# The state chain of an RWKV-7 / dilated attention layer: chain steps issued with a raised priority, the other VectorE and ScalarE work of a step behind the step's two copies

## The chip, the cores and the metric

One core of a Trainium2 chip runs the whole layer in one launch. The metric is the device time of one execution in microseconds (us), median of three runs. Four engines matter: TensorE (PE in the profile; its weight loads are a row of their own, PEld), VectorE (DVE), ScalarE (ACT) and GpSimd (POOL). Each takes its instructions in the order in which the built program has them. SyncE (SP) issues most DMAs.

## What is computed

A decoder layer on 1024 tokens of width 1024, all in float32. One RMS norm and one input projection feed two branches: 16 heads of RWKV-7 time mixing, and 16 heads of attention over three dilated windows. Both are gated by SiLU, joined by one output projection, added to the input and normed again. The change touches only the recurrence of the time mixing:

```python
def rwkv7_time_mix(p_shift, gate, w0, w_up, a0, a_up, k_k, k_a, r_k, ln_x_w, ln_x_b):
    ...
    def step(state, inp):
        r_t, w_t, k_t, v_t, av_t, bv_t = inp
        sa = jnp.einsum('bhvk,bhk->bhv', state, av_t)
        state = (state * w_t[:, :, None, :] + sa[..., None] * bv_t[:, :, None, :]
                 + v_t[..., None] * k_t[:, :, None, :])
        return state, jnp.einsum('bhvk,bhk->bhv', state, r_t)
    ...
    _, y = lax.scan(step, s0, xs)
    ...

def reference(x, norm_w, w_in, mu_shift, ...):
        xn = rms_norm(h, norm_w)
        p = jnp.einsum('bsd,dn->bsn', xn, w_in.astype(jnp.float32))
        ...
        y_rwkv = rwkv7_time_mix(...)
        y_att = mixed_dilated_attention(p[..., ATT0:ATT_GATE0], p[..., ATT_GATE0:])
        mix = jnp.concatenate([y_rwkv, y_att], axis=-1)
        h = h + jnp.einsum('bsm,md->bsd', mix, w_out.astype(jnp.float32))
    return rms_norm(h, final_norm_w).astype(x.dtype)
```

## The kernel before

**Stages.** `rwkv` (L291) does the time mixing, then `attention` and `project_out` follow. The input projection is one long stream of 128x512 matmuls (`stream`, tiles `pq`, L187; three products per weight tile, since each float32 factor is split in two). It is a generator, and every stage draws a few of its matmuls between its own work (`advance`).

**Units and slots.** The time mixing is cut into 16 units: 8 pairs of heads times 2 halves of the sequence, each unit 8 chunks of 64 tokens. The loop over `p` at L341 works on four units at once: unit p+2 is prepared (`prepare`, `products`), p+1 is inverted (`late`, `invert`), p is chained (`chain`), p-1 is finished (`finish`). An iteration has 24 slots (`NSLOT`). A slot runs the steps put into it, the chain step first, then draws 4 matmuls of the projection.

**The chain.** A unit has 24 chain steps, three per chunk. Each ends in a pair of copies out of PSUM: VectorE takes head 0, ScalarE takes head 1, ScalarE behind VectorE.

- `first`: `z<-Sd` (state times keys), copies to `zd`; then two matmuls into `T` that no step waits for at once.
- `second`: `z<-zd` with the inverted matrix `U`, copies to `ud`, scaled by `rn`.
- `third`: `T<-ud`, copies to `Sd`, scaled by the decay: the state of the next chunk. Then `z<-Vd` opens the next `z`.

So a chain step is: matmul, VectorE copy, ScalarE copy, next matmul. The copies are L654 and L655 (`zd`), L657 and L658 (`ud`, `Sd`).

**The inversion.** `U` of a unit comes from `invert`: 15 columns of small VectorE operations (L568, L570: tiles `TB`, `UB`), a trip through DRAM (L577, L581), then four rounds m1 to m4 of small matmuls with ScalarE copies behind each (m1: L596, L599; m2: L606, L610 and the VectorE transpose L611; m3: L619, L622; m4: L628, L631). The second chain step of a unit, `z<-zd`, reads `U`, so it can't run before the last copy of m4.

**What sets the order.** The program is traced in the order of the slots, and a list scheduler then places it: on each engine it takes, of what is ready by its own reckoning of time, the instruction with the highest priority, and priority is the order of tracing. The engines then run that list in order. The lines that this hangs on:

```python
                if dC:
                    put(enumerate(self.chain(dC, get(p + 1) if dC["h"] == 0 else None)))
                ...
                for s in range(NSLOT):
                    for f in ev[s]:
                        f()
                    self.advance(n)
```

Of the kernel before, what the change touches and what calls it, by code (L numbers as in the profile page):

```python
# [12 lines left out]
AF = mybir.ActivationFunctionType  # L13
# [16 lines left out]
ATTG0 = 7296  # L30
NSLOT = 3 * NC_
AHEAD = 120
OFILL = 8
WARM = (4, 0)
V_AT = (-2, 3, -1)
# [18 lines left out]
class Kern:  # L54
# [135 lines left out]
    def stream(self, jobs):  # L190
# [3 lines left out]
        for i, (_, halves, take) in enumerate(jobs):  # L194
# [9 lines left out]
                yield  # L204
            w = wn

    def advance(self, n):
        for _ in range(n):
            next(self.flow, None)
        self.taken += n  # L210
# [80 lines left out]
    def rwkv(self, pairs=range(NPAIR), apairs=range(NPAIR)):  # L291
        nc = self.nc
        with ExitStack() as ctx:
            P = lambda n, b=1, s=None: self.pool(n, b, s, ctx)
            self.ps_a = P("ps_a", 1, PSUM)
            self.ps_z = P("ps_z", 1, PSUM)
            self.ps_y = P("ps_y", 1, PSUM)
            self.ps_tr = P("ps_tr", 1, PSUM)
            self.mid = P("mid", 2)
            self.inv = P("inv", 1)  # L300
            self.pers = pers = P("pers")
            self.lng = P("lng", 3)
            self.dpool = P("dpool", 2, bass.MemoryType.DRAM)
            self.carry = pers.tile([128, 25], F32, name="carry")
            self.Us = [pers.tile([128, NC_ + 1, C], F32, name=f"U{i}") for i in range(2)]
            self.Vds = [pers.tile([128, NC_, 2, HD], F32, name=f"Vd{i}") for i in range(2)]
            self.Sds = [pers.tile([128, 2, HD], F32, name=f"Sd{i}") for i in range(2)]
            self.llo = [pers.tile([128, 128], F32R, name=f"llo{i}") for i in range(2)]
            self.zds, self.uds = ([pers.tile([128, 2, HD], F32, name=f"{nm}{i}") for i in range(2)] for nm in ("zd", "ud"))
            for u in self.Us + self.Vds + self.Sds + self.zds + self.uds:  # L310
                nc.gpsimd.memset(u, 0.0)
            for u in self.llo:
                nc.gpsimd.memset(u.bitcast(F32), 0.0)
            self.ARs = [pers.tile([128, NC_ * 192 + 2], F32, name=f"AR{i}") for i in range(3)]
            for a in self.ARs:
                nc.gpsimd.memset(a[:, NC_ * 192:], 0.0)
                a = self.c192(a)
                for e in range(2):
                    er = slice(e * 64, e * 64 + 64)
                    nc.gpsimd.tensor_copy(out=a[er, :, 0], in_=bc(self.ident[er, er].unsqueeze(1), (64, NC_, 64)))  # L320
            self.d0 = pers.tile([128, 2, C + 1], F32, name="d0")
            nc.gpsimd.memset(self.d0, 1.0)
            nc.gpsimd.memset(self.d0[:, :, C:C + 1], 0.0)
            bank = lambda p, tag: lambda: p.tile([128, 4, 128], F32, name="xq", tag=tag)
            ba = [bank(self.ps_a, "pa0"), bank(self.ps_a, "pa1")]
            tags = ("MV", "MV", "MV", "TU", "TU", "BK")
            for _ in self.prep_x(0, self.lng, tags, [bank(self.ps_proj, "proj")] * 2 + ba):
                pass
            units = [dict(h=h, pr=pr) for pr in pairs for h in range(2)]
            for i, d in enumerate(units):  # L330
                d["AR"], d["Vd"] = self.ARs[i % 3], self.Vds[i % 2]
            N = len(units)
            self.flow = self.stream(self.jobs(units, apairs))
            next(self.flow)
            self.taken = 1
            self.params(self.lng.tile([P_N, 128], F32, name="rows", tag="TU"),
                        self.ps_tr.tile([128, P_N], F32, name="prm_ps", tag="tr"))
            self.advance(6 * KT - 1)
            get = lambda n: units[n] if 0 <= n < N else None
            self.lora_w(units[0])  # L340
            for p in range(-2, N):  # L341
                dA, dI, dC, dF = get(p + 2), get(p + 1), get(p), get(p - 1)
                ev = [[] for _ in range(NSLOT)]
                put = lambda steps: [ev[s].append(f) for s, f in steps]
                if dC:
                    put(enumerate(self.chain(dC, get(p + 1) if dC["h"] == 0 else None)))
                if dF:
                    put(self.finish(dF))
                if dI:
                    put(self.late(dI))  # L350
                    put(self.invert(dI, self.Us[(p + 1) % 2]))
                if dA:
                    lag = WARM[p + 2] if p < 0 else 0
                    put([(n + lag, f) for n, f in self.prepare(dA) + self.products(dA)])
                if get(p + 3) and get(p + 3)["h"] == 0:
                    ev[12].append(lambda d=get(p + 3): self.lora_w(d))
                elif get(p + 3):
                    get(p + 3)["lw"] = get(p + 2)["lw"]
                if p == -2:
                    px = self.prep_x(1, self.lng, tags, ba)  # L360
                    for s in range(4):
                        ev[s].append(lambda: [next(px, None) for _ in range(2)])
                    ev[4].append(lambda: [None for _ in px])
                n = 5 if p < 0 else 2 if dA is not None and get(p + 3) is None else 4
                for s in range(NSLOT):
                    for f in ev[s]:
                        f()
                    self.advance(n)
            for _, f in self.finish(units[-1]):
                f()  # L370

# [262 lines left out]
    def chain(self, d, nxt):  # L634


        nc = self.nc
        V, S, G = nc.vector, nc.scalar, nc.gpsimd
        h, pr = d["h"], d["pr"]
        er = [slice(0, 64), slice(64, 128)]  # L640
        t = {}
        f2 = lambda ap: ap.rearrange("p a b -> p (a b)")
        mm = lambda out, w, x, start, stop: nc.tensor.matmul(out, lhsT=w, rhs=f2(x), start=start, stop=stop,  # L643
                                                             skip_group_check=True)

        def values(c):

            t["z"] = self.ps_z.tile([128, 2, 128], F32, name="z")
            mm(t["z"][0:66, 0], d["MV"][:, c * 192 + 128:c * 192 + 194], d["Vd"][:, c], True, False)

        def spread(out, q, scale):

            if scale is None:
                V.tensor_copy(out=out[er[0], 0], in_=q[0:64, 0:64])  # L654
                S.copy(out=out[er[1], 1], in_=q[0:64, 64:128])  # L655
            else:
                V.tensor_scalar(out=out[er[0], 0], in0=q[0:64, 0:64], scalar1=scale[0], scalar2=None, op0=ALU.mult)  # L657
                S.activation(out=out[er[1], 1], in_=q[0:64, 64:128], func=AF.Copy, scale=scale[1])  # L658

        def first(c):  # L660
            AR = d["AR"]
            if c == 0:
                values(c)
            if c % 4 == 0:
                d["T", c // 4] = self.ps_y.tile([128, 4, 128], F32, name=f"T{c // 4}")
            Sd, T, zd = self.Sds[c % 2], d["T", c // 4][:, c % 4], self.zds[c % 2]
            mm(t["z"][0:66, 0], AR[:, c * 192 + 128:c * 192 + 194], Sd, False, True)
            spread(zd, t["z"][:, 0], None)
            mm(T, d["MV"][:, c * 192:c * 192 + 128], d["Vd"][:, c], True, False)
            mm(T, AR[:, c * 192:c * 192 + 128], Sd, False, False)  # L670

        def second(c):
            mm(t["z"][0:66, 1], f2(d["U"])[:, c * 64:c * 64 + 66], self.zds[c % 2], True, True)
            spread(self.uds[c % 2], t["z"][:, 1], [d["rn"][0:64, c:c + 1], d["rn1"][:, c:c + 1]])

        def third(c):
            T = d["T", c // 4][:, c % 4]
            if c == 5:
                self.heads_out(d, 0)
            mm(T, f2(d["TU"][:, c])[:, 0:128], self.uds[c % 2], False, True)  # L680
            if c == NC_ - 1 and nxt is None:
                G.memset(self.Sds[0], 0.0)
                return
            dec, n = (nxt["dec"], 0) if c == NC_ - 1 else (d["dec"], c + 1)
            spread(self.Sds[(c + 1) % 2], T, [dec[:, e, n:n + 1] for e in range(2)])
            if n:
                values(n)
        return [lambda f=f, c=c: f(c) for c in range(NC_) for f in (first, second, third)]
# [411 lines left out]
```

## Time and profile before

| what | value |
|---|---|
| time, median of 3 runs | 1586.47 us (1586.15 to 1588.06) |
| the profiled execution: time, span | 1586.58 us, 1584.9 us |
| TensorE busy over the span | 1492.5 us (94%) |
| VectorE, ScalarE, GpSimd busy | 64%, 56%, 34% |
| granted clock | 0.993 of full speed |
| stage of the chain | about 128 to 875 us |

The chain stage takes nearly half of the span. The rows below are of that stage. A group of instructions "x2" on PE is one float32 matmul in two passes. The busy time of PE is modelled at its end and matmuls overlap, so the distance from one start to the next says more than the durations.

### The profile page before, as it was taken

To read this page: it belongs to the slowest core of one execution; us is meant where nothing else is said; L and a number is where in the kernel's file an instruction comes from. 1 tells how busy PE (TensorE), PEld (TensorE's weight loads), DVE (VectorE), ACT (ScalarE), POOL (GpSimd) and SP (SyncE) were. 2 spreads that over 40 slices of the span, in tenths; PEclk is the share of its full clock that TensorE was granted. 3 is DMA by queue.
4 is the path that set the end of the run, shared out by engine and by line. 5 is a ranking of instruction groups with operands and counts; after the bars stand their busy time and mean duration, and the time that the engine had idled before them with its cause. 6 is when DMAs were issued, how large, how long until landed. Compare 5 with 4: busy or idle time off the path is not lost.

```text
span 1584.9 us, 29112 instructions
## 1 busy us (share of the span) xinstructions
PE 1492.5 (94%) x10721; PEld 1211.0 (76%) x10721; DVE 1014.7 (64%) x2686; ACT 892.7 (56%) x2080; POOL 532.9 (34%) x668
## 2 busy tenths in 40 slices
PE   5889999999999999999999999999999999999997
PEld 4677777777777777777677788888888888787886
DVE  5866767677666676666743557676675766856234
ACT  5546666666656666566654456556565555645231
POOL 5443132222222221232211433443333334355542
PEclk9999999999999999999999999999999999999999
DMA  6121111111111111111111201111111111436452
GB/s 195 56 67 38 34 40 42 35 45 28 39 45 33 46 39 26 47 31 45 31 40 35 68 28 34 39 50 34 34 34 41 47 48 47 157 103 193 134 166 99
DMA packets 178829, 94.87 MB, mean 60 GB/s; under 512 B 58413, under 2 KB 164606, under 8 KB 178686
## 3 DMA queue, kind: packets, MB, share of 16 engines
q1 hardware_dynamic: 174942, 86.19, 19.6%
q10 hardware_dynamic: 3744, 6.82, 1.3%
q8 instruction: 84, 1.38, 0.4%
q14 instruction: 59, 0.48, 0.1%
HBM read 75.01 MB, written 17.83 MB: 59 GB/s over the span
## 4 chain that ended last, share of the span: by engine, by line
PE 66%; DVE 18%; ACT 9%; issue 4%; POOL 1%; DMA 1%; DVEq 0%; SPq 0%; ACTq 0%; POOLq 0%
PE pq L187 31%; PE oq L984 10%; PE T L643 4%; PE z L643 3%; PE o L930 3%; PE pa L527 2%; PE mp L857 2%; PE sp L890 2%; DVE I L422 1%; PE sp L910 1%; PE sp L909 1%; ACT zt L724 1%; DVE TB L568 1%; ACT ud L658 1%; DVE UB L570 1%
## 5 line engine op out<-in xcount | busy, mean ns | idle before, releaser
L187 PE MATMUL pq<-xh,wh 128*128 128x512 f32 x1040 | 430.6, 414 | 0.0
L187 PE MATMUL pq<-xl,wh 128*128 128x512 f32 x1040 | 414.7, 399 | 0.0
L187 PE MATMUL pq<-xh,wl 128*128 128x512 f32 x1040 | 291.8, 404 | 0.0
L179 POOL TENSOR_TENSOR wl<-wraw,wh 128x512 fp32r<-128x512 f32 x138 | 181.1, 1328 | 173.9 <-issue 46.3
L187 PEld LDWEIGHTS pq<-xh,wh 128*128 128x128 f32 x1040 | 197.0, 190 | 32.6 <-issue 0.2
L187 PEld LDWEIGHTS pq<-xl,wh 128*128 128x128 f32 x1040 | 197.4, 190 | 31.2 <-DVE xl L166 0.2
L187 PEld LDWEIGHTS pq<-xh,wl 128*128 128x128 f32 x1040 | 187.8, 190 | 33.0
L918 POOL TENSOR_TENSOR pl<-p,ph 128x512 fp32r<-128x512 f32 (+2 forms) x96 | 102.0, 1068 | 202.7 <-ACT ph L917 182.4
L984 PE MATMUL oq<-ow,qr 128*128 128x512 f32 x512 | 162.2, 395 | 1.2 <-ACT ow L965 0.6
L859 DVE CUSTOM_DVE_ANT_0 mp<-mp,maskq 128x512 f32<-128x512 f32 (+1 forms) x192 | 105.5, 570 | 68.0 <-PE mp L857 59.5
L913 ACT ACTIVATE p<-p 128x512 f32<-128x512 f32 (+2 forms) x144 | 64.6, 452 | 103.8 <-DVE p L912 103.0
L979 POOL TENSOR_TENSOR vr<-kr,qr 128x512 fp32r<-128x512 f32 (+2 forms) x68 | 90.4, 1335 | 80.9 <-ACT qr L978 74.0
L984 PEld LDWEIGHTS oq<-ow,qr 128*128 128x128 f32 x512 | 95.9, 188 | 23.0 <-ACT ow L965 1.0
L984 PE MATMUL oq<-ow,vr 128*128 128x512 f32 x256 | 101.2, 395 | 1.9 <-POOL vr L979 1.9
L178 ACT CAST wh<-wraw 128x512 fp32r<-128x512 f32 x138 | 79.7, 618 | 40.6 <-PE pq L187 30.9
L978 ACT CAST qr<-kr 128x512 fp32r<-128x512 f32 (+2 forms) x68 | 40.2, 594 | 94.3 <-PE oq L984 53.1
L912 DVE TENSOR_TENSOR p<-sp,maskt 128x512 f32<-128x512 f32 (+2 forms) x144 | 65.3, 457 | 42.9 <-PE sp L910 41.4
L643 PEld LDWEIGHTS T<-ud,TU 128*128 128x128 f32 x256 | 39.6, 188 | 56.2 <-ACT ud L658 51.8
L643 PE MATMUL T<-ud,TU 128*128 128x128 f32 x256 | 59.4, 314 | 22.7 <-ACT ud L658 22.1
L657 DVE TENSOR_SCALAR Sd<-T,dec 64x64 f32<-64x64 f32 x120 | 33.0, 275 | 66.8 <-PE T L643 65.0
L658 ACT ACTIVATE ud<-z,rn 64x64 f32<-64x64 f32 x128 | 39.4, 308 | 56.5 <-DVE ud L657 54.9
L658 ACT ACTIVATE Sd<-T,dec 64x64 f32<-64x64 f32 x120 | 36.9, 308 | 57.0 <-DVE Sd L657 55.6
(235 smaller groups left out, 3126.6 us busy)
## 6 DMA issues: line engine op xcount, KB each, us to landing
wraw<-in_w_in_dram SPq DMA_DIRECT2D x138, 256.0 KB, 3.0
kr<-mixd SPq DMA_DIRECT2D x60, 256.0 KB, 3.0
oraw<-in_w_out_dram SPq DMA_DIRECT2D x16, 512.0 KB, 5.2
xt<-in_x_dram SPq DMA_DIRECT2D x8, 512.0 KB, 3.8
ld<-TU SPq DMA_DIRECT2D x32, 128.0 KB, 2.7
mixd<-zt SPq DMA_DIRECT2D x16, 256.0 KB
mixd<-gt SPq DMA_DIRECT2D x16, 256.0 KB, 2.2
xr<-in_x_dram ACTq DMA_DIRECT2D x16, 256.0 KB, 2.8
```

Of the source, the lines that this page charges most:

```text
L178: nc.scalar.copy(out=wh[:, ks], in_=raw)
L179: nc.gpsimd.tensor_tensor(out=wl[:, ks], in0=raw, in1=wh[:, ks].bitcast(F32), op=ALU.subtract)
L187: return [lambda i=i, a=a, b=b: self.nc.tensor.matmul(q, lhsT=a, rhs=b, start=(i == 0), stop=(i == len(ops) - 1)) for i, (a, b) in enumera ...
L643: mm = lambda out, w, x, start, stop: nc.tensor.matmul(out, lhsT=w, rhs=f2(x), start=start, stop=stop, skip_group_check=True)
L658: S.activation(out=out[er[1], 1], in_=q[0:64, 64:128], func=AF.Copy, scale=scale[1])
L859: V.tensor_tensor_reduce(out=mp[:, :kn], in0=mp[:, :kn], in1=self.maskq[:, v0:v0 + kn], op0=ALU.add, op1=ALU.max, scale=1.0, scalar=-3e38, ...
L912: V.tensor_tensor(out=p[:, :qn], in0=sp[:, :qn], in1=self.maskt[:, u0:u0 + qn], op=ALU.add)
L913: S.activation(out=p[:, :qn], in_=p[:, :qn], func=AF.Exp)
L918: G.tensor_tensor(out=pl[:, :qn], in0=p[:, :qn], in1=ph[:, :qn].bitcast(F32), op=ALU.subtract)
L930: nc.tensor.matmul(oc, lhsT=v, rhs=w[:, :qn], start=(first and i == 0), stop=(last and i == len(prods) - 1), skip_group_check=True)
L979: nc.gpsimd.tensor_tensor(out=ml, in0=raw, in1=mh.bitcast(F32), op=ALU.subtract)
L984: nc.tensor.matmul(q, lhsT=m[:, i], rhs=v, start=(k == 0 and j == 0), stop=(k == 15 and j == 2))
```

## The change

Three edits. First, every chain step is traced under a priority raised by 90 places (`urgent`, `AHEAD_OF`), so that the scheduler treats its instructions as if they stood 90 instructions earlier. Second, the two copies of a chain step are kept (`self.copies`), and everything that the same slot traces behind the chain step on VectorE gets an ordering edge to the VectorE copy, and everything on ScalarE one to the ScalarE copy (`issue_after`): it may not stand ahead of that copy in its engine's list. The edge orders the issue and adds no wait. The draws of the projection in the slot (`advance`) are inside as well, so the `shift` and `gate` operations that they bring are held by the same edges; matmuls and GpSimd's work are not. Third, where a unit has no state copy (the last step of every second unit), the list of copies is empty.

```diff
+AHEAD_OF = 90
...
+    def urgent(self, f):
+
+        with self.tc.high_priority(offset=AHEAD_OF):
+            f()
...
                 if dC:
-                    put(enumerate(self.chain(dC, get(p + 1) if dC["h"] == 0 else None)))
+                    for s, f in enumerate(self.chain(dC, get(p + 1) if dC["h"] == 0 else None)):
+                        ev[s].append(lambda f=f: self.urgent(f))
...
                 for s in range(NSLOT):
-                    for f in ev[s]:
-                        f()
-                    self.advance(n)
+                    with ExitStack() as order:
+                        for i, f in enumerate(ev[s]):
+                            f()
+                            if dC and i == 0:
+                                for ins in self.copies:
+                                    order.enter_context(self.tc.issue_after(ins.ins))
+                        self.advance(n)
...
             if scale is None:
-                V.tensor_copy(out=out[er[0], 0], in_=q[0:64, 0:64])
-                S.copy(out=out[er[1], 1], in_=q[0:64, 64:128])
+                a = V.tensor_copy(out=out[er[0], 0], in_=q[0:64, 0:64])
+                b = S.copy(out=out[er[1], 1], in_=q[0:64, 64:128])
...
+            self.copies = [a, b]
...
             if c == NC_ - 1 and nxt is None:
+                self.copies = []
                 G.memset(self.Sds[0], 0.0)
                 return
```

No instruction is added or taken away on any engine: PE keeps 8051 matmuls, VectorE 2688 instructions, ScalarE 2084, GpSimd 673, SP 575. From the 4848th matmul on, the order on PE is the same again, so only the chain stage is another. Two places show how.

**A chain step in the middle of a unit (the fourth chunk of the seventh unit).** On PE before, the matmuls of steps `first` and `second` of this chunk (`T_4772` is the unit's first `T`, `bq` and `pa` are other units' work), with the line numbers of the kernel before:

```order
1223 L643 MATMUL z<-Sd_123,AR_142 66x128
1224 L643 MATMUL T_4772<-Vd_120,MV 128x128
1225 L643 MATMUL T_4772<-Sd_123,AR_142 128x128
1226 L506 MATMUL bq<-bh,bdr 128x512
1227 L506 MATMUL bq<-bl,bdr 128x512
1228 L187 MATMUL pq<-xh_79,wl 128x512 x6
1229 L643 MATMUL z<-zd_127,U_118 66x128
1230 L187 MATMUL pq<-xh_79,wl 128x512
1231 L527 MATMUL pa_5039<-AR_144,BK 128x128
1232 L527 MATMUL pa_5040<-AR_144,BK 128x128
```

Now, on PE at the same steps (the line numbers are 1 to 13 higher, `tq` and `zq` are other units' work):

```order
1239 L188 MATMUL pq<-xh_78,wh 128x512
1240 L654 MATMUL z<-Sd_123,AR_142 66x128
1241 L654 MATMUL T_4772<-Vd_120,MV 128x128
1242 L654 MATMUL T_4772<-Sd_123,AR_142 128x128
1243 L188 MATMUL pq<-xl_80,wh 128x512
1244 L654 MATMUL z<-zd_127,U_118 66x128
1245 L188 MATMUL pq<-xh_78,wl 128x512 x4
1246 L416 MATMUL zq<-lx_342,lhi_4516 128x512
1247 L417 MATMUL zq<-lx_342,llo_124 128x512
1248 L416 MATMUL aq<-lx_343,lhi_4517 128x512
```

Between `z<-Sd` and `z<-zd` stood two `bq` and six `pq`; one `pq` is left there, and four stand behind `z<-zd`.

On VectorE before, the small operations of the group norm (`rs_w`, `gr`) and `Y` stood behind the `zd` copy of this step and ahead of its `ud` copy:

```order
760 L654 COPY zd_127<-z 64x64
761 L449 RECIPROCAL rn<-rn 128x8
762 L78 TENSOR_TENSOR rs_w<-rs_w,rs_x 128x8
763 L79 SCALAR_TENSOR_TENSOR gr<-rs_w,gr 128x8
764 L77 TENSOR_TENSOR rs_w<-gr 128x8
765 L78 TENSOR_TENSOR rs_w<-rs_w,rs_x 128x8
766 L79 SCALAR_TENSOR_TENSOR gr<-rs_w,gr 128x8
767 L77 TENSOR_TENSOR rs_w<-gr 128x8
768 L78 TENSOR_TENSOR rs_w<-rs_w,rs_x 128x8
769 L79 SCALAR_TENSOR_TENSOR gr<-rs_w,gr 128x8
770 L713 TENSOR_TENSOR Y<-Y,gr 128x512
771 L657 TENSOR_SCALAR ud_129<-z,rn 64x64
```

Now small operations of the norm and of the inversion's columns (`TB`, `UB`) stand between the state copy (`Sd`) and the `zd` copy of the same step:

```order
751 L668 TENSOR_SCALAR Sd_123<-T_4772,dec 64x64
752 L78 TENSOR_TENSOR rs_w<-gr 128x8
753 L579 TENSOR_TENSOR TB<-UB,AB 64x28
754 L79 TENSOR_TENSOR rs_w<-rs_w,rs_x 128x8
755 L581 TENSOR_TENSOR UB<-UB,TB 64x14x2
756 L80 SCALAR_TENSOR_TENSOR gr<-rs_w,gr 128x8
757 L579 TENSOR_TENSOR TB<-UB,AB 64x15
758 L78 TENSOR_TENSOR rs_w<-gr 128x8
759 L581 TENSOR_TENSOR UB<-UB,TB 64x15
760 L79 TENSOR_TENSOR rs_w<-rs_w,rs_x 128x8
761 L80 SCALAR_TENSOR_TENSOR gr<-rs_w,gr 128x8
762 L665 COPY zd_127<-z 64x64
```

So ten small operations now stand ahead of the `zd` copy that feeds row 1244 of PE, and behind the `Sd` copy that feeds its row 1240; before, the nine of the group norm stood behind that `zd` copy.

**The end of the fifth unit and the start of the sixth.** On PE before, from m4 (the sixteen `x` matmuls) on:

```order
1002 L628 MATMUL x_4111<-U_119,Xs 32x32 x16
1003 L187 MATMUL pq<-xh_79,wh 128x512
1004 L187 MATMUL pq<-xl_81,wh 128x512
1005 L187 MATMUL pq<-xh_79,wh 128x512
1006 L187 MATMUL pq<-xl_81,wh 128x512
1007 L643 MATMUL z<-zd_127,U_118 66x128
1008 L187 MATMUL pq<-xh_79,wl 128x512 x6
1009 L643 MATMUL T_3909<-ud_129,TU 128x128
1010 L187 MATMUL pq<-xh_79,wl 128x512 x2
1011 L643 MATMUL z<-Vd_121,MV 66x128
1012 L643 MATMUL T_4182<-Vd_121,MV 128x128
1013 L496 MATMUL tq<-ident,BK 128x128 x4
```

Now, from m3 on:

```order
1037 L630 MATMUL x_4111<-UT,TU 32x32 x16
1038 L188 MATMUL pq<-xh_79,wh 128x512
1039 L188 MATMUL pq<-xl_81,wh 128x512
1040 L188 MATMUL pq<-xh_79,wh 128x512
1041 L188 MATMUL pq<-xl_81,wh 128x512
1042 L639 MATMUL x_4111<-U_119,Xs 32x32 x16
1043 L188 MATMUL pq<-xh_79,wh 128x512
1044 L188 MATMUL pq<-xl_81,wh 128x512
1045 L188 MATMUL pq<-xh_79,wh 128x512
1046 L188 MATMUL pq<-xl_81,wh 128x512
1047 L654 MATMUL z<-zd_126,U_119 66x128
1048 L188 MATMUL pq<-xh_79,wl 128x512 x6
```

Before, m4 stood ahead of the last steps of the old unit (`z<-zd_127`, `T<-ud_129`), and the reader of `U_119`, the `z<-zd` of the new unit, came 18 rows behind m4, in row 1020. Now the new unit's first `z<-Sd` is already done (its `T_4182` matmuls stand in rows 1022 and 1031), and the reader `z<-zd_126` stands four `pq` behind m4.

## Rows read from the trace of the kernel before

**Rows 1.** Windows: us, then busy time of each engine (instructions), PEclk, DMA share, GB/s

```profile
128.00:875.00 747.00, 703.78 (x6732) 551.73 (x6731) 493.38 (x1528) 455.46 (x1202) 183.07 (x308) 1.00 0.16 38
875.00:1584.90 709.90, 691.16 (x3351) 580.14 (x3349) 435.06 (x971) 368.44 (x744) 295.56 (x264) 0.99 0.25 76
```

**Rows 2.** Chain of waits, 400 to 450 us: start, us, nine `pq` in a row

```profile
447.87 2.09 PE pq L187 x9
```

**Rows 3.** Timeline, 420 to 434 us: start, us, instruction, count [idle before <-releaser]

```profile
426.14 0.17 DVE L77 TENSOR_TENSOR rs_w<-gr 128x8 f32<-128x8 f32 x1
...
426.34 0.17 DVE L78 TENSOR_TENSOR rs_w<-rs_w,rs_x 128x8 f32<-128x8 f32 x1
...
430.79 0.38 PE L643 MATMUL z<-Sd,AR 128*66 128x128 f32 x2
...
431.01 0.39 PE L643 MATMUL T<-Vd,MV 128*128 128x128 f32 x2
...
431.23 0.39 PE L643 MATMUL T<-Sd,AR 128*128 128x128 f32 x2
```

**Rows 4.** Timeline, 500.5 to 514 us: chain copies behind free engines

```profile
501.16 0.38 PE L643 MATMUL z<-zd,U 128*66 128x128 f32 x2
...
501.47 0.68 PE L596 MATMUL xq<-U,LT 32*16 32x16 f32 x64
501.58 0.28 DVE L657 TENSOR_SCALAR ud<-z,rn 64x64 f32<-64x64 f32 x1 [1.38 <-PE z L643]
501.89 0.31 ACT L658 ACTIVATE ud<-z,rn 64x64 f32<-64x64 f32 x1 [1.45 <-DVE ud L657]
...
510.62 0.38 PE L643 MATMUL z<-Sd,AR 128*66 128x128 f32 x2
...
511.04 0.22 DVE L654 COPY zd<-z 64x64 f32<-64x64 f32 x1 [0.41 <-PE z L643]
...
511.29 0.20 ACT L655 COPY zd<-z 64x64 f32<-64x64 f32 x1 [0.79 <-DVE zd L654]
```

**Rows 5.** Tile T, matmuls `T<-ud`: duration min/median/max in ns, first and last start

```profile
L643 PE MATMUL T<-ud,TU x256: 270/275/377, 132.3 to 874.8; 128*128 128x128 f32 x128
```

**Rows 6.** Waits of PE, 128 to 876 us: us in total, times, longest us

```profile
PE T L643 <- ACT ud L658: 22.1, 39, 1.0
PE z L643 <- ACT zd L655: 9.2, 11, 1.3
PE z L643 <- ACT Sd L658: 7.4, 15, 0.7
```

**Rows 7.** Timeline, 433 to 446 us: a late state copy

```profile
435.07 1.50 ACT L724 COPY zt<-yq 64x256 f32<-64x256 f32 x4
...
435.62 0.28 DVE L657 TENSOR_SCALAR Sd<-T,dec 64x64 f32<-64x64 f32 x1
...
436.82 0.81 ACT L461 ACTIVATE ta<-ta,hk 128x512 f32<-128x512 f32 x1
...
437.66 0.31 ACT L658 ACTIVATE Sd<-T,dec 64x64 f32<-64x64 f32 x1
...
438.02 0.43 PE L643 MATMUL z<-Sd,AR 128*66 128x128 f32 x2 [0.61 <-ACT Sd L658]
```

**Rows 8.** Timeline, 500.5 to 514 us: the rounds m2 to m4 of an inversion

```profile
506.04 1.06 ACT L610 COPY U<-dq 16x128 f32<-16x128 f32 x4 [0.44 <-PE dq L606]
...
507.13 0.71 DVE L611 STREAM_TRANSPOSE UT<-U 128x512 f32<-128x512 f32 x1 [0.98 <-ACT U L610]
...
509.75 0.76 ACT L622 COPY Xs<-x 32x256 f32<-32x256 f32 x2 [0.21 <-PE x L619]
...
511.38 0.69 PE L628 MATMUL x<-U,Xs 32*32 32x32 f32 x32
...
512.12 0.74 ACT L631 COPY U<-x 32x256 f32<-32x256 f32 x2 [0.62 <-PE x L628]
```

More of the change, by code (lines that the diff above doesn't have):

```diff
@@ L653, in spread @@
             if scale is None:
-                V.tensor_copy(out=out[er[0], 0], in_=q[0:64, 0:64])
-                S.copy(out=out[er[1], 1], in_=q[0:64, 64:128])
-            else:
-                V.tensor_scalar(out=out[er[0], 0], in0=q[0:64, 0:64], scalar1=scale[0], scalar2=None, op0=ALU.mult)
-                S.activation(out=out[er[1], 1], in_=q[0:64, 64:128], func=AF.Copy, scale=scale[1])
+                a = V.tensor_copy(out=out[er[0], 0], in_=q[0:64, 0:64])
+                b = S.copy(out=out[er[1], 1], in_=q[0:64, 64:128])
+            else:
+                a = V.tensor_scalar(out=out[er[0], 0], in0=q[0:64, 0:64], scalar1=scale[0], scalar2=None, op0=ALU.mult)
+                b = S.activation(out=out[er[1], 1], in_=q[0:64, 64:128], func=AF.Copy, scale=scale[1])
+            self.copies = [a, b]
         def first(c):
```

## The prediction, made before the change was timed

> **What bounds the kernel now.** I read the windows first, to see which engine fills the stage that the change touches, then the spacing of matmuls in the chain of waits and the timeline, then the tile view of the chain's matmuls, then PE's waits and the timeline around one of them.
>
> In the chain stage PE is busy 703.78 of 747.0 us (94%), VectorE 493 (66%), ScalarE 455 (61%); behind it PE is busy 691 of 710 us [rows 1]. From the 4848th matmul on the order is the same, so the change is worth what it does to the stage, and a us of PE there is a us of the end.
>
> How much of the stage is waiting? Starts tell more than busy time. A `pq` follows a `pq` after 2.09/9 = 0.232 us [rows 2], a chain matmul of two passes takes 0.22 [rows 3]. A change between these and the small matmuls of an inversion costs about 0.09 more: the second pass of `z<-zd` starts at 501.27, `xq` 0.20 later instead of 0.11 [rows 4]. I gave every matmul of the stage such a cost, the other kinds by their own starts. From the first `T<-ud` to the last, the order before holds 682 us of PE work; the trace takes 874.8 - 132.3 = 742.5 [rows 5]. So 60.6 us are waiting. The wait rows show 22.1 + 9.2 + 7.4 = 38.7 of it, all for the ScalarE copy that ends a chain step [rows 6]; the rest is gaps that modelled ends hide.
>
> [...]
>
> Why is a copy late? In one example the `Sd` copy on VectorE ends at 435.90, but its partner on ScalarE starts at 437.66: ScalarE was in four `zt` copies and `ta`, which its list had ahead. `z<-Sd` follows 0.05 us behind it and PE had stood 0.61 us [rows 7].
>
> With free engines a copy pair takes little. `z<-zd` at 501.16, VectorE at 501.58, ScalarE from 501.89 to 502.20, plus the 0.05: 1.09 us from one chain matmul to the next. For the lighter `zd` pair: 510.62 to 511.49, plus 0.05: 0.92 us [rows 4]. The order before gives 1.79 us of PE work a step (682 over 381), so on the mean there is time in hand; what counts is which steps have less.
>
> **The change part by part.** It adds and removes no instruction. What moves is the chain: it runs ahead of the other work until it meets the inversion. So it can be placed the moment its copies are reckoned ready, where before it often stood behind projection matmuls and had time in hand.
>
> *Cover.* For each of 360 steps (units 2 to 16; the first is startup) I counted from the order the PE work P between two chain matmuls, and the VectorE and ScalarE work D and A between the matching copies. A copy falls behind by the larger of D - P and A - P; the next step takes that up with P less 1.09 (or 0.92), and PE waits for what is left. An example is shown under the change: ten small VectorE operations 0.20 us apart [rows 3] and the `zd` copy make D = 2.2; PE has `T<-ud`, `z<-Vd`, one `tq` and three `pq` = 1.35 us, so the copy is 0.85 late; the next step has 3 x 0.22 + 0.23 = 0.89 us of PE work against a bare 0.92. PE waits about 0.9 us. Before, the norm's operations lay behind the copy and beside 2.5 us of PE work.
> Summed: 14.9 us before and 30.3 after, +15.4. Of it 6.0 is steps with less PE work than the bare latency (11 before, 55 now), 8.7 is VectorE, 0.7 ScalarE.
>
> *Switches.* The order on PE breaks into more pieces: by the same count 77 more changes between kinds of matmul, at 0.09 us: +6.9.
>
> *Inversion.* Its result is now read four `pq` behind m4. Need: 0.69 + 0.05 + 0.74 + 0.05 = 1.53 us from the start of m4 [rows 8]; there: 0.5 + 0.1 + 4 x 0.232 = 1.53. Nothing in hand, nothing lost. From m2 to m3 stand eight `pq`, 1.96 us with the switch, against tail and start of 0.32 and the copies and transpose of 1.80 (506.04 to 507.84) [rows 8]: short by 0.15-0.2. Fifteen units: +3. If one other ScalarE or VectorE operation of 0.7 us slips into each of the three links, it is 2.1 x 15 = 31 instead.
>
> *Prompter copies.* My rule gives 14.9 of the 60.6 us. The other 45.7 come from work that itself waits for another engine while a copy stands behind it; the trace shows this for the order before alone. Ends: all of it goes, or it grows by half, 23 us, as fewer steps have time in hand. The 7.4 us of `z<-Sd` [rows 6] are mostly the place of [rows 7]; in the new order the same run (`Ux`, `dec`, `zt`, `ta`, two `wh`: 5.4 us) stands ahead of an `ud` copy with 7.4 us of PE work in two steps beside it, so I take these as gone. Of the remaining 38.3 I take the share by which the sum of all overruns D - P and A - P falls (93.2 to 84.8, 9%): 3.4. Together -10.8.
>
> The edges put everything else of a slot behind its copies. What stands behind a late copy: `shift` and `gate`, which free the `pq` banks; the column work; the split of weights. A bank is wanted again 24 matmuls later (six slots), so I cost this at nothing; if that cover went, one late `shift` costs PE its 0.7 us. SP's DMAs and GpSimd have no edge; 5 of SP's 575 instructions and 78 of GpSimd's 673 change places, which I cost at nothing, since no wait of PE on either stands in the wait rows of the stage.
> [...]
>
> Sum: 15.4 + 6.9 + 3 - 10.8 = +14.5. The profiled execution took 1586.58 us (span 1584.9 and 1.7 around it), the median is 1586.47; so 1601.
>
> **Rivals.**
> *The copies become prompt (faster).* For it: all 38.7 us of PE's waits end at a copy queued behind other work [rows 6, 7], and the largest VectorE runs between copies get smaller (overruns -9%). If three quarters of the 45.7 go, 34 us, against 25.3 of loss: 1578; if all goes, 1566. Against it: in the new order 55 steps have no time in hand, so what is left of the lateness reaches PE whole. It decides the other way once more than 25.3 of the 45.7 are gone.
> *The parts cancel.* Cover lost and copies gained are within 3 us of each other: 1584 to 1590. For it: PE work is the same and the stage is 92% PE work.
> *The inversion becomes the bound (slower than forecast).* The 31 us above in place of 3: 1629. For it: nothing is in hand at m4. Against: ScalarE's list has almost nothing else between the links.
> That the change does nothing is out: the orders differ all through the stage.
>
> **How the numbers follow.** Forecast 0.47 (its own range 1592 to 1612), prompt copies 0.31, cancelled 0.12, inversion 0.10. What a measurement of this kernel can tell from no change is 0.2%, about 3 us. Slower: 0.47 + 0.10 = 0.57, less a little that the forecast's low side gives up: 0.56. Faster 0.32, same 0.12. The range goes from 1564, all lateness gone (1566), to 1624, the growth of 23 us on the forecast; the full inversion case lies just outside.
>
> **What would show it.** In the profile after: the distance from first to last `T<-ud`, 742.5 now, should be about 757. Waits of `z<-zd` for `zd` should grow most from 9.2 us, in every unit at the fourth chunk; `z<-Sd` for `Sd` should nearly vanish. VectorE's and ScalarE's busy time stay. If the `zd`, `ud` and `Sd` copies start within 0.1 us of their matmul's end in most steps and PE's waits together fall under 38.7, the first rival is right and my cover rule is wrong. If `z<-zd` waits once a unit for over 1 us right behind m4, it is the inversion.

## The result and the profile after

The changed kernel takes 1607.08 us (median of four runs, 1605.73 to 1610.16) against 1587.26 us for the kernel before on the same chip: a ratio of 1.0128, with a 95% interval of 1.0111 to 1.0146. It is about 20 us slower; 1601 was forecast. The profiled execution took 1606.17 us (span 1604.5).

The windows of the stage and of what follows, as in [rows 1] (us, busy time of PE, PEld, DVE, ACT and POOL with instructions, PEclk, DMA share, GB/s):

```profile
128.00:895.00 767.00, 722.37 (x6718) 547.72 (x6717) 498.35 (x1553) 459.19 (x1204) 190.13 (x310) 1.00 0.16 37
895.00:1604.50 709.50, 691.81 (x3360) 580.80 (x3358) 429.09 (x955) 368.23 (x743) 293.56 (x262) 1.00 0.25 76
```

The matmuls `T<-ud`, which answer to [rows 5]:

```profile
L654 PE MATMUL T<-ud,TU x256: 270/275/378, 127.4 to 888.0; 128*128 128x128 f32 x128
```

From the first to the last they now take 760.6 us instead of 742.5: +18.1. The chain begins 4.9 us earlier, and 716.5 us follow on its last `T<-ud` instead of 710.1, since projection matmuls were left over: +6.4. Together 18.1 - 4.9 + 6.4 = 19.6, the difference of the two spans.

PE's waits from 128 to 896 us, against [rows 6] (us in total, times, longest):

```profile
PE T L654 <- ACT ud L669: 14.3, 20, 0.8
PE z L654 <- ACT zd L666: 9.0, 25, 0.5
PE pa L538 <- DVE BK L474: 8.7, 6, 1.5
PE z L654 <- ACT Sd L669: 3.6, 6, 1.4
```

In these rows the chain's own waits fell from 38.7 to 26.9 us, and `pa` for `BK` is new. So the 18 us are not in the wait rows.

The rows do not hold all waiting, though. They leave out the shortest idle times (in the changed kernel 0.06 to 0.14 us in front of `z<-Sd`, several times in every unit), and the modelled end of the matmul before can hide a wait altogether. Counted by starts instead (for each matmul that reads a chain copy, its distance from the start of the matmul before it, less the lowest tenth of that distance for the same two kinds of matmul over all fourteen traces), the chain's readers waited 59.1 us before and 64.5 us now: `z<-zd` 15 and now 19, `T<-ud` 31 and 25, `z<-Sd` 13 and 20. All but 0.6 us of it lies, in both kernels, at readers that begin within 0.1 us of their ScalarE copy. So by starts the chain waits 5.4 us longer, not 11.8 less.

The window from first to last `T<-ud` shows where the 18 us are. Before:

```profile
132.30:874.80 742.50, 700.32 (x6711) 549.00 (x6711) 489.74 (x1516) 452.86 (x1195) 180.53 (x305) 1.00 0.16 38
```

After:

```profile
127.40:888.00 760.60, 715.97 (x6690) 542.50 (x6690) 494.14 (x1537) 457.83 (x1200) 189.88 (x308) 1.00 0.16 36
```

PE stands idle for 742.50 - 700.32 = 42.2 us before and 44.6 after, only 2.4 more. It is *busy* 15.7 us longer, with 21 fewer matmul records (24 `pq` less). Some of that is waiting under modelled ends, as just counted. One place shows what else it is. In the timeline of PE in the changed kernel (start us, us, instruction, count), a round of an inversion (`dq`, 64 small matmuls, whole in all 16 units before) is cut in three by chain matmuls:

```profile
467.32 0.38 PE L654 MATMUL z<-zd,U 128*66 128x128 f32 x2
467.63 0.37 PE L617 MATMUL dq<-Xs,UT 16*16 16x16 f32 x28
467.93 0.49 PE L654 MATMUL T<-Vd,MV 128*128 128x128 f32 x2
468.34 0.27 PE L617 MATMUL dq<-Xs,UT 16*16 16x16 f32 x14
468.67 0.49 PE L654 MATMUL T<-ud,TU 128*128 128x128 f32 x2
469.00 0.38 PE L654 MATMUL z<-Vd,MV 128*66 128x128 f32 x2
469.31 0.32 PE L617 MATMUL dq<-Xs,UT 16*16 16x16 f32 x22
```

Counted over the whole trace, PE changes between the small matmuls (`xq`, `dq` and `x` of the inversion, `pa`) and the others 260 times before and 344 times after; between the first and the last `T<-ud` it is 244 and 320. `dq` stands in 50 pieces.

### The profile page after: what moved, and what is told of

Read it like the earlier page. It is cut to its first block, busy times and chain, and to the rows that moved or that the text cites. A ratio compares the mean times of both kernels' runs of the same rounds, so it can differ in the third digit from the quotient of the medians.

```text
span 1604.5 us, 29162 instructions
## 1 busy us (share of the span) xinstructions
PE 1511.5 (94%) x10721; PEld 1207.4 (75%) x10721; DVE 1011.9 (63%) x2686; ACT 895.5 (56%) x2080; POOL 538.2 (34%) x668
## 4 chain that ended last, share of the span: by engine, by line
PE 65%; DVE 16%; ACT 13%; issue 3%; POOL 1%; DMA 1%; SPq 0%; DVEq 0%; ACTq 0%; POOLq 0%
PE pq L188 31%; PE oq L997 10%; PE T L654 4%; PE z L654 4%; PE o L943 3%; PE mp L870 2%; PE sp L903 2%; DVE TB L579 2%; DVE UB L581 1%; ACT Vd L501 1%; DVE I L433 1%; PE pa L538 1%; ACT zt L737 1%; PE sp L923 1%; PE sp L922 1%
## 5 line engine op out<-in xcount | busy, mean ns | idle before, releaser
L188 PE MATMUL pq<-xh,wh 128*128 128x512 f32 x1040 | 426.2, 410 | 0.0
L188 PE MATMUL pq<-xl,wh 128*128 128x512 f32 x1040 | 420.6, 404 | 0.0
L179 ACT CAST wh<-wraw 128x512 fp32r<-128x512 f32 x138 | 80.3, 617 | 42.2 <-PE pq L188 33.6
L668 DVE TENSOR_SCALAR ud<-z,rn 64x64 f32<-64x64 f32 x128 | 35.0, 273 | 100.2 <-PE z L654 99.0
L654 PE MATMUL T<-ud,TU 128*128 128x128 f32 x256 | 59.2, 313 | 16.9 <-ACT ud L669 14.3
L538 PE MATMUL pa<-AR,BK 64*128 64x128 f32 x512 | 56.0, 306 | 18.0 <-DVE BK L474 16.8
L654 PEld LDWEIGHTS T<-ud,TU 128*128 128x128 f32 x256 | 39.8, 188 | 43.1 <-ACT ud L669 38.7
```

Source lines behind the costliest of these rows:

```text
L179: nc.scalar.copy(out=wh[:, ks], in_=raw)
L188: return [lambda i=i, a=a, b=b: self.nc.tensor.matmul(q, lhsT=a, rhs=b, start=(i == 0), stop=(i == len(ops) - 1)) for i, (a, b) in enumera ...
L538: nc.tensor.matmul(q[e][:, b], lhsT=BK[er[e], c], rhs=AR[er[e], c * 192 + 64:c * 192 + 192], start=True, stop=True)
```

## The experiments

Twelve kernels. The numbers of the table are worked out alike from every trace: the stretch from first to last `T<-ud`; PE's busy time in it; the idle rest; the changes between small and other matmuls, here over the whole trace; and the clock loss, which is 1 minus the granted clock, summed over the stretch in steps of 2 us.

| kernel | ratio to before (95%) | first to last `T<-ud` | PE busy | idle | changes | clock loss |
|---|---|---|---|---|---|---|
| before | 1 | 742.5 | 700.3 | 42.2 | 260 | 0 |
| changed | 1.0128 (1.0111 to 1.0146) | 760.6 | 716.0 | 44.6 | 344 | 1.7 |
| e1_priority | 1.0099 (1.0082 to 1.0116) | 754.7 | 718.7 | 36.0 | 374 | 1.7 |
| e2_edges | 1.0214 (1.0199 to 1.0229) | 775.3 | 713.5 | 61.9 | 304 | 6.8 |
| e3_ahead30 | 1.0300 (1.0284 to 1.0315) | 783.9 | 730.1 | 53.8 | 510 | 0 |
| e4_behind40 | 1.0286 (1.0270 to 1.0301) | 787.3 | 720.2 | 67.1 | 318 | 5.1 |
| e5_copies | 0.9982 (0.9973 to 0.9991) | 740.5 | 696.3 | 44.2 | 224 | 0 |
| e5_matmuls | 1.0324 (1.0310 to 1.0338) | 794.6 | 732.1 | 62.5 | 348 | 17.1 |
| e6_spare_inv | 1.0214 (1.0200 to 1.0228) | 775.7 | 714.1 | 61.6 | 282 | 6.9 |
| e7_spare_prep | 1.0123 (1.0109 to 1.0137) | 758.8 | 721.1 | 37.7 | 372 | 1.7 |
| e8_not0 | 1.0129 (1.0115 to 1.0143) | 757.0 | 708.1 | 48.9 | 318 | 1.7 |
| e8_inv | 1.0365 (1.0344 to 1.0385) | 807.4 | 748.8 | 58.6 | 326 | 32.4 |
| e9_copies_edges | 1.0142 (1.0128 to 1.0155) | 762.2 | 703.3 | 58.9 | 220 | 15.4 |
| e10_whole | 1.0118 (1.0089 to 1.0148) | 757.7 | 704.8 | 52.9 | 268 | 10.2 |

**One part at a time.** `e1_priority` drops the edges, `e2_edges` the priority:

```diff
 e1_priority
-                            if dC and i == 0:
-                                for ins in self.copies:
-                                    order.enter_context(self.tc.issue_after(ins.ins))
 e2_edges
-                        ev[s].append(lambda f=f: self.urgent(f))
+                        ev[s].append(f)
```

> The raised priority alone, without the ordering edges. Theory (cover): the time is lost because a chain step that is issued as early as it can be has less PE work between its copies and the matmul that reads them. The rule of the prediction, applied to the instruction lists of this kernel, sums 38.5 us of PE waiting against 14.9 before and 30.3 in the changed kernel, and 5 us more of matmul and switching: with the same 10.8 us off for prompter copies as in the forecast, 1587 + 23.6 + 5 - 10.8 = 1605 us, about as slow as the changed kernel (1607). Rival (edges): the priority is harmless and the queueing of the other VectorE and ScalarE work costs the time: 1580 to 1590 us, and the new wait of pa for BK (8.7 us) is gone.

> The ordering edges alone, at the old priority. Theory (cover): the rule sums 25.8 us of PE waiting against 14.9 before, and 4 us more of matmul and switching; only 17 steps fall short of the bare latency of the copies, against 11 before and 55 in the changed kernel. Less than half of the loss: 1590 to 1600 us. Rival (edges): all of the loss is here, 1605 us or more, with waits of pa for BK and of other matmuls for work that stands behind the copies. Second rival (prompt copies): the edges make the copies prompt and the priority spoils it: 1570 to 1583 us.

Measured: 1601.24 us (+15.5) and 1620.34 us (+34.6), beside 1585.71 for before. Each part alone loses; the edges alone lose more than the whole change. The theory came near with the first (1605 expected) and missed the second (1590 to 1600). `pa` still waits for `BK` in the priority alone, 2.2 us; in the edges alone it does not, so its 8.7 us in the changed kernel take both parts.

**Less priority, and lower priority.** `AHEAD_OF = 30` with the edges, and -40 without them.

> The changed kernel with the chain raised by 30 places instead of 90. Theory (cover): 21 short steps instead of 55 and a rule sum of 28.5 us against 30.3, but 14 us more of PE work falls between the first and the last chain step: 1600 to 1610 us, so little is won by a third of the rise. Rival (the size of the rise decides): about a third of the way from the edges alone to the changed kernel.

> The opposite sign: no edges, the chain's priority lowered by 40 places. Theory (cover): time in hand grows back, the rule sums 19.6 us (14.9 before, 30.3 after) and the work of VectorE and ScalarE overruns its step less (83.5 us against 93.2 before): 1585 to 1597 us, clearly under the raised priority. Rival (the chain is the bound and must come early): slower than the changed kernel, 1610 to 1630 us, since every chain step comes later.

Measured: 1634.01 and 1631.22 us, both far above what the cover rule gave. A third of the rise is worse than all of it, and the opposite sign loses 45 us. So the rule, which happened to fit the changed kernel, does not predict these kernels, and neither does "early" or "late" as such.

**Copies or matmuls.** `e5_copies` raises the two copies of a chain step and nothing else; `e5_matmuls` raises the matmuls and leaves the copies. Neither has edges.

```diff
 e5_copies, in spread (steps no longer wrapped in urgent)
+            with self.tc.high_priority(offset=AHEAD_OF):
                 ... the two copies ...
 e5_matmuls (steps wrapped in urgent, as in the change)
+            with self.tc.high_priority(offset=-AHEAD_OF):
                 ... the two copies ...
```

> The raised priority on the two copies of a chain step alone, its matmuls at the old priority, no edges: the copies go ahead of other VectorE and ScalarE work, and the matmuls keep their places. Theory (what costs is that the chain's matmuls come early and leave no work between copy and reader): nothing of the loss is here; the work that overruns a step falls to 64 us against 93 before, the steps below the bare latency stay at 10 (11 before), so 1575 to 1587 us. Rival (the moved VectorE and ScalarE work, pa's BK and the inversion's products, costs it, whoever moves it): 1595 us or more, with pa waiting for BK as in the changed kernel.

> The other half: the chain's matmuls raised by 90, the two copies of each step at the old priority, no edges. Theory (early matmuls leave no work in hand): the loss of the raised priority or more, 1605 to 1630 us, since the copies overrun more (201 us against 93). Rival (the copies' places decide): within 10 us of before, 1580 to 1597 us.

Measured: 1583.71 us against 1586.23 (eleven and fifteen runs; 2.5 us faster, and the only kernel here that beats the one before the change), and 1637.79 us. This separates the two halves of the raised priority: the copies' half gains a little, the matmuls' half is what costs. Between `e5_copies` and `e1_priority` only the matmuls' priority differs, and that is some 18 us: 150 more changes, PE busy 22.4 us longer, idle 8.2 us shorter. The readers of `e1_priority` begin within 0.1 us of their ScalarE copy in 245 of 376 chain steps, in `e5_copies` in 172, before in 183, in the changed kernel in 249. So the time in hand is lost as forecast, but it does not come out as waiting (by starts the readers wait 54.8 us in `e1_priority` and 60.4 in `e5_copies`). Nor does `e5_copies` gain by shorter waits, since they were 59.1 us in the kernel before; what fell are the changes, by 36. In `e5_copies` the groups stay whole (`pa` in 32 groups of 16, `xq` in 16 of 64).

**The edges: what stands ahead of the copies.** `e6_spare_inv` is `e2_edges` with `invert`'s steps traced outside the edges, `e7_spare_prep` the changed kernel with `prepare` and `products` outside:

```diff
+                            if f in spared:
+                                with order.pop_all():
+                                    pass
+                                f()
+                                for ins in self.copies if dC else []:
+                                    order.enter_context(self.tc.issue_after(ins.ins))
+                                continue
```

> The edges alone, with the inversion's instructions left out of them. In the edges alone T<-ud waited 48.4 us for ud (22.1 before), and ud's copy stood in the longest of these behind the inversion's products, TB<-UB,AB: a product queued behind the copies of one step is still running when the next step wants VectorE. Theory (that product): 1587 to 1603 us, waits of T<-ud back under 30 us. Rival (any work queued behind the copies does the same): 1613 us or more, another tile in TB's place.

> The changed kernel, with the preparation of the unit after next (its BK, TU, MV and the products) left out of the edges. Theory (in the changed kernel the edges cost 6 us beyond the raised priority, by pa's new waits for BK, which the edges hold up): about the time of the raised priority alone, 1598 to 1604 us, pa's waits for BK inside the chain back at 2 us or less. Rival (pa's wait comes of the raised priority and has nothing to do with the edges): 1605 to 1610 us, the waits as in the changed kernel.

Measured: 1619.74 us, unchanged against `e2_edges`, and 1606.03 us. In `e6_spare_inv` the products did not leave: the longest waits for `ud` now have the other product, `UB<-UB,TB`, ahead of the copy. The waits of `T<-ud` fell from 48.4 to 40.7 us only, and those for `Sd` rose from 3.1 to 12.1. So it moved little of what it was meant to move and leaves its question open. In `e7_spare_prep` no wait of `pa` for `BK` is left inside the stage:

```profile
PE T L663 <- ACT ud L678: 14.6, 40, 1.0
PE z L663 <- ACT zd L675: 10.0, 16, 0.7
PE z L663 <- ACT Sd L678: 9.8, 24, 1.4
```

Without these edges the wait is gone, as the theory said; the time falls into the rival's range all the same. Taking its 8.7 us away shortened the stretch by 1.8 us only: the waits for `Sd` rose from 3.6 to 9.8 and the changes from 344 to 372.

`e9_copies_edges` is `e5_copies` with the edges of the change:

> Only the copies raised, the chain's matmuls at the old priority, and the edges of the changed kernel. Theory (edges make work that stands behind one step's copies late, and that work then stands ahead of the next step's copies, whatever the copies' priority): as slow as the edges alone, 1610 to 1622 us, with T<-ud waiting over 40 us. Rival (the edges lose because copies at the old priority leave their order to chance): 1583 to 1595 us.

Measured: 1607.42 us, 22 more than before and about 25 more than the same kernel without edges (by the ratios). The time lies between the two ranges, nearer the theory's. `T<-ud` waits 37.4 us for `ud` (27.0 in `e5_copies`). Once a unit, fourteen times in all, one such wait takes 1.78 to 2.43 us. The one near 230 us in the timeline of PE (in brackets: idle before it, and the releaser):

```profile
229.18 0.40 PE L188 MATMUL pq<-xl,wh 128*128 128x512 f32 x1
231.62 0.61 PE L654 MATMUL T<-ud,TU 128*128 128x128 f32 x2 [2.05 <-ACT ud L670]
232.03 0.63 PE L654 MATMUL z<-Vd,MV 128*66 128x128 f32 x2
232.31 0.78 PE L188 MATMUL pq<-xh,wh 128*128 128x512 f32 x1
232.89 0.63 PE L188 MATMUL pq<-xl,wh 128*128 128x512 f32 x1
```

VectorE at the same time:

```profile
228.14 1.16 DVE L581 TENSOR_TENSOR UB<-UB,TB 64x28 f32<-64x28 f32 x1
229.34 1.24 DVE L579 TENSOR_TENSOR TB<-UB,AB 64x39 f32<-64x39 f32 x1
230.61 0.19 DVE L581 TENSOR_TENSOR UB<-UB,TB 64x39 f32<-64x39 f32 x1
230.83 0.20 DVE L579 TENSOR_TENSOR TB<-UB,AB 64x48 f32<-64x48 f32 x1
230.96 0.27 DVE L669 TENSOR_SCALAR ud<-z,rn 64x64 f32<-64x64 f32 x1
```

And GpSimd:

```profile
227.92 1.34 POOL L180 TENSOR_TENSOR wl<-wraw,wh 128x512 fp32r<-128x512 f32 x1 [3.28 <-ACT wh L179]
229.20 0.09 POOL L223 MEMSET shtmp<- 128x1 f32 x1
229.26 1.26 POOL L180 TENSOR_TENSOR wl<-wraw,wh 128x512 fp32r<-128x512 f32 x1
```

Two products that take 0.2 us elsewhere take 1.2 each, exactly while GpSimd subtracts, and the `ud` copy stands behind both. So the order did not only put work ahead of a copy, it put it beside the wrong neighbour. Of the 480 products, 19 take over 0.6 us before (22.1 us in all), 19 in `e5_copies`, 24 in `e1_priority`, 31 in the changed kernel (36.6 us), 33 in `e2_edges` and in `e9_copies_edges` (39.8 us). In all fourteen traces every product of over 0.6 us lies beside a GpSimd TENSOR_TENSOR. No run took GpSimd's work away from there.

And a second loss follows on the wait. The windows of this stretch (last but two columns: the granted clock):

```profile
228.00:230.00 2.00, 1.57 (x8) 0.92 (x6) 1.93 (x3) 1.73 (x5) 2.00 (x3) 1.00 0.00 0
230.00:232.00 2.00, 0.38 (x2) 0.38 (x3) 1.83 (x8) 0.70 (x3) 0.52 (x1) 0.96 0.50 141
232.00:234.00 2.00, 2.00 (x8) 1.69 (x7) 1.34 (x7) 1.37 (x3) 0.00 (x0) 0.50 0.41 121
234.00:236.00 2.00, 2.00 (x12) 1.83 (x11) 1.17 (x5) 0.20 (x1) 0.00 (x0) 0.68 0.00 0
```

PE was busy for 1.57 and then 0.38 of 2 us; behind that the clock is granted at 0.50, and `pq` takes 0.63 us instead of 0.40. That follows nine of the fourteen long waits.

**Was it the start of the unit?** With the chain raised, the list holds 5 to 6 us of projection behind the first `z<-Sd` of a unit, until `U` is there.

```diff
 e8_not0 (e1_priority, the first chunk's three steps not raised)
-                        ev[s].append(lambda f=f: self.urgent(f))
+                        ev[s].append((lambda f=f: self.urgent(f)) if s > 2 else f)
 e8_inv (e1_priority, the inversion raised as well)
-                    put(self.invert(dI, self.Us[(p + 1) % 2]))
+                    put([(s, lambda f=f: self.urgent(f)) for s, f in self.invert(dI, self.Us[(p + 1) % 2])])
```

> The raised priority without edges, but not for the first of a unit's eight chunks (its three chain steps keep the old priority). With all steps raised, the first z<-zd of a unit has 4.9 to 6.0 us of PE work ahead of it in the list (1.1 to 2.4 before), because it needs the inverse U, which is not raised; that work is missing between the other 23 steps. Theory (that hole is where the time in hand went): the hole is 2.4 us here, the rule sum 17.9 us against 38.5 with all raised, so 1580 to 1592 us. Rival (any matmul of the chain that is raised loses, hole or not): 56 steps stay below the bare latency, as many as in the changed kernel, so 1595 us or more.

> The raised priority without edges, with the inversion raised by the same 90 places, so that U is there when the raised chain asks for it. Theory (the hole): it closes (2.5 us), the rule sum is 15.7 us and 19 steps are below the bare latency, but 10 us more of matmul and switching falls into the chain's stretch: 1583 to 1597 us. Rival (the raised matmuls lose in any case): 1600 us or more.

Measured: 1606.07 and 1644.30 us. The hole theory fell with both; raised matmuls lose without the hole too. `e8_inv` is the slowest kernel of all, and its 32.4 us of clock loss are half of the 65 us by which its stretch is longer.

**Groups kept whole.** `e1_priority` with only the matmuls of m1 to m4 raised above the chain:

```diff
+            with self.tc.high_priority(offset=200):
                 for c in range(NC_):
                     ... the matmuls of xq, dq, x ...
```

> The raised priority without edges, with the matmuls of the inversion's four steps (xq, dq, x) raised above the chain (by 200), so that the raised chain no longer splits their groups; nothing else of the inversion is raised. In the trace of the raised priority alone dq's 64 matmuls stand in 51 pieces in all instead of 16 whole groups, and PE changes between small-tile and other matmuls 374 times against 260 before. Theory (the splitting is what the raised matmuls cost): about as many changes as before, 250 to 290, and the loss of 15.5 us shrinks by some 10 to 14 us: 1586 to 1593 us. Rival (copies have less work to hide behind, split or not): the rule sums 28.4 us against 14.9 before and 38.5 in the raised priority alone: 1596 to 1606 us, with dq whole again.

Measured: 1606.24 us (six runs, 1593.74 to 1611.11); by the time this speaks against the theory, by the mechanism for it. The changes fall from 374 to 268, `dq` is whole in all 16 units, and PE's busy time in the stretch falls from 718.69 to 704.81 us:

```profile
121.40:879.10 757.70, 704.81 (x6697) 548.54 (x6697) 505.10 (x1545) 454.79 (x1195) 185.04 (x308) 0.99 0.16 36
```

That is 13.9 us off, although the clock costs 8.5 us more here. But 16.9 us of idle time came instead, most of it `T<-ud` waiting for `ud` (34.1 us, up from 11.2): the order that keeps the groups whole is another order, and copies in it stand behind operations on `ks` of 0.7 us. The spread of the runs follows the clock: 1593.74 us at a mean granted clock of 0.993, 1611.11 at 0.982. At 0.993, the clock of the kernel before (1586.56), the loss is 7 us, half of `e1_priority`'s; that is a single run.

**The account.** A least-squares fit through the fourteen rows of the table gives: stretch = 661.9 + 0.145 x changes + 1.11 x clock loss + 1.00 x idle. It misses by 4 us (root mean square), at most by 8 (`e9_copies_edges`, `e10_whole`). It is a fit, not a measurement of each term. Two pairs without any clock loss price a change directly: before to `e5_copies` 36 changes fewer and PE busy 4.0 us less (0.11 each), before to `e3_ahead30` 250 more and 29.8 us more (0.12 each); these busy times hold hidden waits too. The same work whole and cut shows the price without any. Before, `z<-zd` and a whole `xq` stand between these two `pq` ([rows 4] has both):

```profile
500.93 0.39 PE L187 MATMUL pq<-xl,wh 128*128 128x512 f32 x1
502.08 1.19 PE L187 MATMUL pq<-xh,wl 128*128 128x512 f32 x4
```

In `e4_behind40` the same chain matmul cuts the same group in two:

```profile
157.96 0.40 PE L188 MATMUL pq<-xl,wh 128*128 128x512 f32 x1
158.29 0.45 PE L604 MATMUL xq<-U,LT 32*16 32x16 f32 x36
158.67 0.43 PE L651 MATMUL z<-zd,U 128*66 128x128 f32 x2
159.03 0.37 PE L604 MATMUL xq<-U,LT 32*16 32x16 f32 x28
159.33 0.97 PE L188 MATMUL pq<-xh,wl 128*128 128x512 f32 x3
```

From `pq` to `pq` it is 1.15 us whole and 1.37 cut: 0.22 us for two more changes, 0.11 each.

So the 18.1 us of the changed kernel add up in about this way: 76 more changes at 0.11 to 0.145, 8 to 11 us; the chain's readers by starts, 5.4; `pa`, 8.7 for `BK` less 1.9 that it waited for `MV` before, 7; the clock, 1.7; 24 `pq` less, 5.6 us off. That is some 17 to 19 us. It is read from starts and rows: no run takes the changes away and leaves the rest as it is.

## Why the prediction was right, and where its steps were not

The direction, the size (+14.5 forecast, +19.8 measured) and the range held. The parts did not all hold.

- **Switches: the count right, the price too low.** 77 more changes were counted, and 76 are between the first and the last `T<-ud` (84 in the whole trace); at 0.11 to 0.145 they are 8 to 11 us where 6.9 were forecast. The 0.09 came from one start-to-start distance on entering a group. This is the largest term of the loss.
- **Prompter copies: not borne out.** -10.8 was forecast. The wait rows of the chain fell by 11.8 us, 7.8 of it at `T<-ud` and 3.8 at `z<-Sd`, which was to give nearly all of its 7.4. By starts, the ruler of the prediction's 60.6 us, `z<-Sd` waits 7 us longer and only `T<-ud` less, by 6.
- **Cover: the step that failed as a rule.** Time in hand went away as counted (66 more steps whose reader follows the copy within 0.1 us; 44 more short steps were forecast). The waits of `z<-zd` were to grow most from their 9 us: in the rows they went from 11 to 25 times at the same 9 us, half a us at most, by starts they grew by 4; at the fourth chunk they came in every unit, but 0.45 us and not 0.9. Cover and prompter copies together were forecast at +4.6, and the chain's readers wait 5.4 us longer by starts. That is luck, since neither part came as forecast. And the rule fails as a rule: it put `e2_edges`, `e3_ahead30` and `e4_behind40` at 1585 to 1610 us, and they took 1620 to 1634; for `e1_priority` it summed the most, 38.5 us, and there the readers waited less than before. It weighs lengths of lists; it knows nothing of a product that takes 1.2 us instead of 0.2, nor of a clock granted at 0.50.
- **The test set for the rival** (copies prompt in most steps and waits under 38.7) was met by half: the wait rows are 26.9 us and VectorE's copy starts within 0.1 us of its matmul's end in 264 of 376 steps (225 before), but ScalarE's within 0.1 us of VectorE's in 190 (206 before). So the copies became prompter on VectorE only, and the reader needs both. The test leant on the wait rows, which miss the short waits.
- **Inversion: next to nothing**, where +3 was forecast. Matmuls of the inversion wait 0.4 us in the rows of the whole stage. Its groups were split, which the prediction had under switches.
- **Edges at nothing: wrong in the place, small in the sum.** On top of the raised priority they cost about 5 us (1.0128 against 1.0099; the intervals touch). With them `pa` waits 8.7 us for `BK`; without that wait the kernel is hardly faster (1.0123 against 1.0128, inside each other's interval). On their own they cost 35 us. The prediction did not price that, and the changed kernel has little of it: its longest wait of `T<-ud` is 0.8 us, in `e2_edges` 2.4.
- **First to last `T<-ud`:** 757 forecast, 760.6 found. What lies around it was put at nothing and is +1.5 us.

So the number came out in part because terms erred in opposite directions: the changes were 1 to 4 us too cheap, `pa`'s 7 us and the clock's 1.7 were not foreseen, the inversion's 3 did not come, and 24 `pq` (5.6 us) moved out of the stretch.

## What to carry to other kernels

When a priority moves work on an engine that is 94% busy, look at its busy time and its starts, not at its wait rows alone: here those rows fell while the kernel got slower. PE took longer because raised instructions cut into groups that ran cheaply while whole (0.11 to 0.145 us for each change), and because short waits hide in modelled ends. Raise only what is short and urgent, the copies, and leave the bulk where it is; that was the one variant that gained (0.2%), with fewer changes and no shorter waits. And taking one wait away proves little in a list that is this full: `pa`'s 8.7 us (`e7_spare_prep`) and the 106 changes (`e10_whole`) each went, and other waits took their place.

## What the runs showed of the hardware

- A VectorE product with two operands in SBUF can take 1.2 us instead of 0.2 beside a GpSimd subtraction. In the changed kernel (DVE, then POOL):

```profile
228.07 1.20 DVE L581 TENSOR_TENSOR UB<-UB,TB 64x63 f32<-64x63 f32 x1
229.20 0.21 DVE L665 COPY zd<-z 64x64 f32<-64x64 f32 x1
229.33 1.17 DVE L579 TENSOR_TENSOR TB<-UB,AB 64x60 f32<-64x60 f32 x1
```

```profile
227.92 2.51 POOL L180 TENSOR_TENSOR wl<-wraw,wh 128x512 fp32r<-128x512 f32 x2 [9.19 <-PE tq L507]
```

  The second product ends as GpSimd's two subtractions end (230.50 and 230.43 us; in the rows of `e9_copies_edges` above each product ends within 0.06 us of one subtraction), and the copy out of PSUM between them takes its usual 0.21 us. What holds VectorE up there was not shown.
- Behind nine of the fourteen waits of about 2 us in `e9_copies_edges` the granted clock is halved, to 0.50, for some 3 us (windows above), which loses 15.4 us of its stretch. Before and in `e5_copies` nothing of the stretch is lost to that. So 1.7 us on the mean went behind each of these nine waits, themselves of 2.05 to 2.43 us, and no list of waits shows that.
- A wait is not all that a halved clock follows. Of the 32 us that `e8_inv` loses, 24 belong to three stretches of 13.7 to 20.5 us at a granted clock of 0.50, and PE stood idle for less than 1 us in the 6 us ahead of each. The longest begins at 574.5 us; from 568.5 to 582.4 us PE ran chain matmuls and small groups and no `pq`:

```profile
570.00:574.00 4.00, 3.76 (x83) 2.66 (x83) 1.65 (x4) 1.84 (x5) 2.94 (x4) 1.00 0.45 131
574.00:578.00 4.00, 4.00 (x26) 3.45 (x19) 1.25 (x4) 3.54 (x10) 1.09 (x2) 0.56 0.02 4
578.00:582.00 4.00, 4.00 (x77) 3.12 (x77) 0.49 (x2) 0.32 (x2) 0.69 (x3) 0.50 0.00 0
```
